# TensorE's fixed issue order, ended after the first part of a Conformer layer or kept to the end of the kernel

## The chip, the core and the metric

The kernel runs on one NeuronCore of one Trainium2 chip. The metric is the device time of one execution in microseconds. Three runs before the change gave 2952.1, 2952.1 and 2953.67 us; their median is 2952.1 us.

## What is computed

One inference step of a one-layer streaming encoder, in float32, for a prompt of 2048 frames and a sample of 64 frames (2112 rows, 1024 channels). Cut to what matters here:

```python
h = rms_norm(x, p['norm1_g']) * (1 + sc1) + sh1
z = h @ p['w_in']                                   # first part, with the convolution
...                                                 # and the band attention
conv_out, conv_state = conv_module(u, conv_hist, ..., p['w_conv_out'])
attn_out = o @ p['w_attn_out']
merged = jax.nn.sigmoid(g_conv) * conv_out + jax.nn.sigmoid(g_attn) * attn_out
x = x + gt1 * (merged @ p['w_o'])
h2 = rms_norm(x, p['norm2_g']) * (1 + sc2) + sh2
gate, up = jnp.split(h2 @ p['w_ffn_in'], 2, axis=-1)
x = x + gt2 * ((jax.nn.silu(gate) * up) @ p['w_ffn_out'])
```

The feed-forward width is 2816, which is 22 tiles of 128 channels (NF = 22). Everything from `conv_out` on is the second part of the kernel, and the change concerns this part.

## The kernel before

**Precision.** Every float32 operand of a product is split into a high and a low part (`whi` and `wlo` for weights), and one product is three TensorE matmuls (`mm3`: high x high, high x low, low x high). ScalarE copies the high part, VectorE or GpSimd subtracts to get the low part.

**Two parts.** The first part runs over four blocks of tokens and does the input projection, the convolution and the attention. The second part runs over three blocks of tokens, `CBLOCKS` = rows 0 to 576, 576 to 1344 and 1344 to 2112; they are called s = 0, 1, 2 below. For each block it does, in the order in which the program is written:

- *merge*, in two chunks of two or three token tiles: for each of eight channel tiles, 12 matmuls on the convolution branch and 12 on the attention branch (`ps<-cin` in the profile), then the gates on VectorE and the split into `m`.
- *output projection* (`wo`), after the merge of each chunk: `pw<-m`, per token tile 8 steps of 6 matmuls.
- *residual*, one Python generator per token tile: residual addition, norm, eight TensorE transposes (`pw<-ident,xn` or `pt<-ident,xn`), modulation ("columns"), and then the differences of the four quarters (channel halves x token halves) that the next stage uses. The quarters and their differences are tiles named b11, b21, b22 and t1 to t4; the profile leaves numbers out and calls them `b` and `t`. For the last chunk of block 0 (`by_pe`), three of the additions per tile are done by TensorE, two matmuls each, with a plus or minus identity matrix (`pw<-b,signs`).
- *feed-forward, first product*, as a product of two-by-two blocks with seven sub-products (Strassen's scheme): each of the 22 steps `up(f)` has seven groups of 12 matmuls. For f under 5 (EARLY) two of them are done ahead, in ten groups called `first(f)` and `second(f)`, which read b11 and b21. In `up(f)` the groups come in the order s2 x t2, s3 x t3, s1 x t1, a22 x t4 (all `ps<-t`), then a12 x b21, a11 x b11 of the next f, s4 x b22 (all `ps<-b`). For f = 0, s3 comes before s2.
- *feed-forward, second product*: `pd<-hid` and `pd<-sums`. In blocks 1 and 2 it is in seven sub-products too (`down_pair`, four stages D1 to D4 of 9, 18, 27 and 9 matmuls, one stage after each `next(between)` in `up(f)` for even f), elsewhere plain (`add_down`).

**What sets the order.** The program is written with a tile framework. Before it emits instructions, the framework's scheduler goes through all of them with a timing model and sets the order on each engine: of the instructions that the model holds ready, it takes the one that stands first in the program. Inside `tc.manual_schedule(engines={PE})` it keeps TensorE's instructions in the order of the program and orders only the other engines. On the chip each engine then works through its own list, and waits at an instruction whose operands or whose buffer aren't ready.

The program itself also has a planner, `Stream`: it adds up estimated times per engine (`stream.load`), and `spend()`, called at the end of each `mm3`, lets waiting generators step once their due time is reached (a *lane*; the residual generators are in the lane `turns`, at most one step in 600 ns of estimated TensorE time, two generators open at a time). So the transposes of the residual stand in the program between matmuls of other groups, at places that depend on the planner's estimates. At some points the program drains a lane, that is, emits all that is left in it at once. The place that matters most, in the second part of each block:

```python
for step, f in ((first, 0), (first, 1), (second, 0), (first, 2), (second, 1)):   # L2312
    step(f)
while hs["columns"]:                       # some tile's transposes not emitted yet
    turns.step(turns.gens[0])
W.presum()
if not s:
    W.begin_last()
turns.drain()                              # L2319
W.early = False
for step, f in ((first, 3), (second, 2), (first, 4), (second, 3), (second, 4)):  # L2321
    step(f)
    W.fill()
```

`first(0)`, `second(0)` and `first(2)` use the same PSUM bank (y0), `first(1)` and `second(1)` the bank z0, `first(3)` and `first(4)` banks of the ring of four called gp.

All instructions go through one helper that records them, so the profile shows nearly all of them at line 105; groups are told apart by tile names.

Of the kernel before, what the change touches and what calls it, by code (L numbers as in the profile page):

```python
# [622 lines left out]
def streaming_layer(ctx: ExitStack, tc: tile.TileContext, I, O):  # L623
# [1017 lines left out]
    ordered = ExitStack()  # L1641
# [68 lines left out]
    tail.drain()  # L1710
    stream.flush()
    side.close()
    ordered.close()
    p1.close()


# [185 lines left out]
    for s, (lo, hi) in enumerate(CBLOCKS):  # L1902
# [344 lines left out]
        def add_left(left):  # L2247

            for dst, x1, out in left:
                gps.tensor_tensor(dst, dst, x1, ALU.add)  # L2250
                stream.at(stream.when("pool") + OUT_LAG, lambda out=out, dst=dst: nc.sync.dma_start(out, dst))
                yield stream.when("pool"), {"pool": 500}
# [95 lines left out]
        stream.flush()  # L2348
        if left:
            work.add(add_left(left))  # L2350


_INS = [
# [26 lines left out]
```

## Time and profile before

| | us |
|---|---|
| median of three runs | 2952.1 |
| profiled execution, device time | 2952.32 |
| its span from first to last instruction | 2950.5 |
| TensorE busy in the span | 2890.8 (98%) |
| VectorE, ScalarE, GpSimd busy | 2046.4, 1363.3, 1162.6 |
| first matmul of the second part | at 1174.4 |
| last matmul | at 2944.8 |

Busy time counts a matmul to its modelled end, and successive matmuls overlap; the distance from one start to the next is the better measure of what a matmul takes in a row. "Idle before" an instruction, with an arrow to what released it, is a wait of the engine itself.

### The profile page before, as it was taken

How to read it: one execution, taken by the hardware profiler on the slowest of the kernel's cores; microseconds unless marked ns; L12 is line 12 of the kernel's file. 1: busy time of each engine (PE TensorE's matmuls, PEld its weight loads, DVE VectorE, ACT ScalarE, POOL GpSimd, SP SyncE). 2: the span in 40 equal slices, each digit the busy share in tenths (PEclk: the TensorE clock that was granted, in tenths of full speed). 3: DMA queues.
4: the chain of work that ended last, by engine and by line, in shares of the span. 5: the costliest groups of instructions: out<-in, count | busy, mean ns of one | idle time of the engine just before them, and what ended most of it. 6: DMA issues, size and time to landing. Idle time of an engine off the chain costs nothing.

```text
span 2950.5 us, 44832 instructions
## 1 busy us (share of the span) xinstructions
PE 2890.8 (98%) x16193; PEld 2585.3 (88%) x16193; DVE 2046.4 (69%) x3648; ACT 1363.3 (46%) x2453; POOL 1162.6 (39%) x753
## 2 busy tenths in 40 slices
PE   7999999999999999999999999999999999999999
PEld 5899777887888788888999998999999999999998
DVE  5897788667956885577767746666666557566666
ACT  3345533751465267464334345444444345444442
POOL 1101210111011002454566452366667742465667
PEclk9999999999999999999999999999999999999999
DMA  9989889978995997985444876332333965333333
GB/s 320 316 296 309 279 280 326 295 234 294 290 294 195 308 264 238 282 301 166 143 147 143 277 258 218 96 123 87 114 121 104 337 224 181 97 98 109 115 107 126
DMA packets 467067, 628.04 MB, mean 213 GB/s; under 512 B 36196, under 2 KB 314584, under 8 KB 466845
## 3 DMA queue, kind: packets, MB, share of 16 engines
q1 hardware_dynamic: 452944, 606.11, 63.6%
q10 hardware_dynamic: 13901, 19.08, 1.9%
q8 instruction: 127, 2.08, 0.3%
q14 instruction: 95, 0.78, 0.1%
HBM read 476.53 MB, written 148.54 MB: 212 GB/s over the span
## 4 chain that ended last, share of the span: by engine, by line
PE 46%; DVE 2%; DMA 1%; ACT 1%; issue 1%; POOL 0%; SPq 0%; ACTq 0%; DVEq 0%; POOLq 0%
PE ps L105 28%; PE pd L105 13%; PE pw L105 5%; DVE wlo L105 1%; ACT whi L105 0%; DVE ps L105 0%; DMA cin<-o_d 0%; DMA x<-x_d 0%; DMA wst<-in_w_conv_out 0%; POOL wlo L105 0%; DMA wfo<-in_w_ffn_out 0%; DVE acc L105 0%; DVE sums L105 0%; DVE pw L105 0%; DMA tg<-g_d 0%
## 5 line engine op out<-in xcount | busy, mean ns | idle before, releaser
L105 PE MATMUL ps<-t,whi 128*128 128x384 f32 (+1 forms) x2112 | 501.8, 322 | 3.2 <-DVE u L105 1.1
L105 POOL TENSOR_TENSOR wlo<-wst,whi 128x1024 fp32r<-128x1024 f32 (+1 forms) x159 | 363.4, 2297 | 235.0 <-ACT whi L105 213.6
L105 ACT ACTIVATE whi<-wst 128x1024 fp32r<-128x1024 f32 (+1 forms) x265 | 258.3, 979 | 317.0 <-PE ps L105 127.8
L105 PE MATMUL ps<-b,whi 128*128 128x384 f32 (+1 forms) x1584 | 380.6, 325 | 5.4 <-DVE v L105 2.1
L105 PEld LDWEIGHTS ps<-t,whi 128*128 128x128 f32 x2112 | 367.7, 188 | 10.5 <-ACT u L105 3.3
L105 DVE SCALAR_TENSOR_TENSOR y<-u,wd,y 128x512 f32<-128x512 f32 (+1 forms) x480 | 369.4, 773 | 7.2
L105 PE MATMUL ps<-hh,whi 128*128 128x512 f32 (+2 forms) x992 | 362.6, 365 | 0.1
L105 DVE TENSOR_TENSOR acc<-acc,pd 128x512 f32<-128x512 f32 x482 | 322.0, 684 | 48.4 <-PE pd L105 45.9
L105 PE MATMUL ps<-hh,wlo 128*128 128x512 f32 (+2 forms) x992 | 344.9, 348 | 0.0
L105 PE MATMUL ps<-hl,whi 128*128 128x512 f32 (+2 forms) x992 | 344.3, 347 | 0.0
L105 PE MATMUL ps<-t,wlo 128*128 128x384 f32 (+1 forms) x1056 | 338.2, 321 | 0.0
L105 PE MATMUL pd<-whi,hid 128*128 128x512 f32 x912 | 297.5, 391 | 0.5 <-DVE hid L105 0.3
L105 PEld LDWEIGHTS ps<-b,whi 128*128 128x128 f32 x1584 | 276.8, 188 | 13.6 <-DVE v L105 3.2
L105 ACT ACTIVATE pr<-pr,sm 128x640 f32<-128x640 f32 (+2 forms) x272 | 201.8, 748 | 138.5 <-DVE sm L105 136.6
L105 PE MATMUL ps<-b,wlo 128*128 128x384 f32 (+1 forms) x792 | 256.0, 323 | 0.0
L105 POOL TENSOR_TENSOR r<-t,mhalf 128x1 f32<-128x1 f32 (+2 forms) x68 | 82.3, 1219 | 415.5 <-DVE t L105 383.2
L105 PEld LDWEIGHTS ps<-hh,wlo 128*128 128x128 f32 x992 | 186.4, 188 | 22.7
L105 DVE TENSOR_TENSOR wlo<-wst,whi 128x1024 fp32r<-128x1024 f32 (+1 forms) x106 | 135.6, 1283 | 101.4 <-ACT whi L105 96.8
L105 PEld LDWEIGHTS pd<-whi,hid 128*128 128x128 f32 x912 | 171.1, 188 | 36.9 <-DVE acc L105 1.4
L105 PEld LDWEIGHTS ps<-hh,whi 128*128 128x128 f32 x992 | 187.0, 188 | 18.0 <-issue 2.9
L105 PEld LDWEIGHTS ps<-hl,whi 128*128 128x128 f32 x992 | 187.4, 189 | 14.5 <-issue 1.7
L105 PEld LDWEIGHTS ps<-t,wlo 128*128 128x128 f32 x1056 | 198.1, 188 | 0.8
(233 smaller groups left out, 6299.0 us busy)
## 6 DMA issues: line engine op xcount, KB each, us to landing
whi<-w_din_h SPq DMA_DIRECT2D x72, 512.0 KB, 6.9
wlo<-w_din_l SPq DMA_DIRECT2D x72, 512.0 KB, 7.0
wst<-sum_d SPq DMA_DIRECT2D x131, 256.0 KB, 2.9
wfo<-in_w_ffn_out SPq DMA_DIRECT2D x64, 512.0 KB, 4.1
wmod<-in_w_ada SPq DMA_DIRECT2D x46, 512.0 KB, 9.4
sum_d<-ws SPq DMA_DIRECT2D x88, 256.0 KB, 2.1
wst<-in_w_ffn_in SPq DMA_DIRECT2D x85, 256.0 KB, 3.3
wst<-in_w_in SPq DMA_DIRECT2D x40, 512.0 KB, 6.9
```

The lines of the kernel that those rows point to most:

```text
L105: self.last = f(*args, **kw)
```

## The change

The scope in which TensorE keeps the order of the program was closed at the end of the first part; now it is closed at the end of the kernel. So from the first merge on, TensorE too gets its matmuls and transposes in the order in which the program emits them. The instructions themselves, their operands and their number stay as they are; the other engines are ordered by the scheduler as before.

```diff
     tail.drain()
     stream.flush()
     side.close()
-    ordered.close()
     p1.close()
...
         stream.flush()
         if left:
             work.add(add_left(left))
+    ordered.close()
```

`ordered` is the scope, entered before the first part:

```python
ordered = ExitStack()
ordered.enter_context(tc.manual_schedule(engines={mybir.EngineType.PE}))
```

## The prediction

> **What bounds the kernel now.** I read the page's totals first, then the busy time by stage, then who ended TensorE's idle time in the second part.
>
> ```profile
> span 2950.5 us, 44832 instructions
> PE 2890.8 (98%) x16193; PEld 2585.3 (88%) x16193; DVE 2046.4 (69%) x3648; ACT 1363.3 (46%) x2453; POOL 1162.6 (39%) x753
> PE 46%; DVE 2%; DMA 1%; ACT 1%; issue 1%; POOL 0%; SPq 0%; ACTq 0%; DVEq 0%; POOLq 0%
> ```
> ```profile
> 1174.00:2951.00 1777.00, 1756.41 (x9682) 1626.11 (x9682) 1162.08 (x1934) 792.30 (x1375) 1001.78 (x601) 1.00 0.51 166
> 2000.00:2300.00 300.00, 300.00 (x1580) 281.43 (x1578) 196.03 (x320) 132.68 (x226) 205.30 (x124) 1.00 0.38 117
> ```
> ```profile
> PE ps L105 <- DVE t L105: 2.7, 4, 1.6
> PE ps L105 <- DVE v L105: 2.1, 3, 1.4
> ...
> PE pd L105 <- DVE acc L105: 0.3, 1, 0.3
> ```
> ```profile
> 2944.78 0.39 PE L105 MATMUL pd<-whi,hid 128*128 128x512 f32 x1
> ```
>
> TensorE bounds it. In the second part (first window row; first number after the comma is TensorE's busy time) it is idle for 1777.0 - 1756.4 = 20.6 us, and some 6 us of that lie behind the last matmul (last row). The waits before it are twelve small groups of 0.3 to 2.7 us (first two and last shown). Over 300 us of the feed-forward of block 1 it is never idle. So the change cannot save more than about 15 us, and the question is where the order of the trace differs from that of the program, since a matmul that ran ahead of its turn ran where TensorE would have waited.
>
> **The change part by part.** I compared the trace's sequence of tile names with the code. No work is added or removed; only the place of some matmuls changes.
>
> *Steady feed-forward: nothing.* In blocks 1 and 2 the trace has the program's groups in the program's order, down to one matmul of a22 x t4 that runs ahead of the second half of stage D2:
>
> ```profile
> 2004.26 0.33 PE L105 MATMUL ps<-t,whi 128*128 128x384 f32 x1
> 2004.43 0.39 PE L105 MATMUL pd<-whi,sums 128*128 128x512 f32 x1
> ```
>
> This moves 0.17 us behind instead of ahead, with no wait seen at either place. The transposes of the residual in these blocks stand after whole `mm3` triples, as the planner puts them, so they do not move either.
>
> *Block 0, merge: +1.1 us.* While a merge product waits for VectorE to free its bank, the trace runs five matmuls of the output projection (first two of five, then the released product), and three more from 1203.42 (the first of them):
>
> ```profile
> 1199.80 0.40 PE L105 MATMUL pw<-whi,m 128*128 128x512 f32 x1
> 1200.03 0.41 PE L105 MATMUL pw<-wlo,m 128*128 128x512 f32 x1
> 1201.58 0.54 PE L105 MATMUL ps<-cin,whi 128*128 128x320 f32 x2 [0.44 <-DVE m L105]
> ...
> 1203.42 0.40 PE L105 MATMUL pw<-wlo,m 128*128 128x512 f32 x1
> ```
>
> Start to start such a matmul takes 0.23 us. In program order it comes after the merge; the product still starts at 1201.58, so five fill nothing any more: 5 x 0.23 = 1.1 us. Ends: 0 (VectorE gets there sooner) and 8 x 0.23 = 1.8.
>
> *Block 0, residual of the last chunk: +9 us, the largest term.* Two tiles, A and B, each go through eight transposes, columns, and three additions by TensorE with VectorE and ScalarE work between them. The trace hides these chains under the 120 `first`/`second` matmuls (the 128 of the row are those and 8 additions) and under `up(0)`:
>
> ```profile
> 1287.20:1309.10 21.90, 19.40 (x128) 1.00 1.04 378
> ```
> ```profile
> 1294.36 1.14 ACT L105 ACTIVATE xn<-x,r 128x1024 f32<-128x1024 f32 x1
> 1297.52 1.58 PE L105 MATMUL pw<-ident,xn 128*128 128x128 f32 x13
> 1302.01 0.63 PE L105 MATMUL pw<-b,signs 128*128 128x512 f32 x2
> 1303.97 0.74 PE L105 MATMUL pw<-b,signs 128*128 128x512 f32 x2
> 1306.26 0.63 PE L105 MATMUL pw<-b,signs 128*128 128x512 f32 x2
> 1306.99 0.63 PE L105 MATMUL pw<-b,signs 128*128 128x512 f32 x2
> 1309.19 0.63 PE L105 MATMUL pw<-b,signs 128*128 128x512 f32 x2
> 1311.64 0.63 PE L105 MATMUL pw<-b,signs 128*128 128x512 f32 x2
> 1316.15 0.40 PE L105 MATMUL ps<-t,whi 128*128 128x288 f32 x1 [1.13 <-DVE u L105]
> 1419.27 0.30 PE L105 MATMUL ps<-t,wlo 128*128 128x288 f32 x1
> 1419.40 0.29 PE L105 MATMUL ps<-b,whi 128*128 128x288 f32 x1
> 1420.23 0.53 PE L105 MATMUL ps<-t,whi 128*128 128x288 f32 x2 [0.54 <-ACT u L105]
> ```
>
> The program does not interleave them so. Following the planner's sums by hand (it counts 288/2.4 ns per matmul, so 0.36 us per triple, and lets one residual step go at each tick), I find A's transposes after about 48 of the first 60 `b` matmuls and B's not yet emitted when the 60 are out. Then the loop on `hs["columns"]` emits all that is left of A, then B's transposes, and `turns.drain()` B's additions; only then come the other 60. A matmul of 288 takes 1419.40 - 1419.27 = 0.13 us. So: A's transposes when `xn` is there at 1295.5, the first 60 out at about 1298.1; A's first addition 2.9 us after its transposes (as from 1299.10 to 1302.01 in the trace), at 1299.4; the second 2.0 and the third 2.3 us later (1302.01, 1303.97, 1306.26), at 1303.7; B's transposes until 1305.2; its additions at 1308.1, 1310.3 and 1312.7 (1306.99, 1309.19, 1311.64); the other 60 until 1321.1; two groups of `up(0)`, 3.1 us, and a short wait for `u`: s1 x t1 starts at 1324.8. In the trace it starts at 1316.15 with 13 matmuls of `up(1)`, 1.7 us, already done. Loss: 8.7 + 1.7 = 10.4 us. If the chain's four steps between additions shrink to 1.5 us, since VectorE and ScalarE have less beside it, it is 7.4. I take 9. Ends: 3.5, if B's transposes do fall within the first 60 (saves 3.9 us), and 12, if A's don't either.
>
> *The clock after that: +3 us.* In these 15 us TensorE would work some 4 us. Once in the trace it was as little loaded:
>
> ```profile
> 1170.40:1173.80 3.40, 2.26 (x13) 1.58 (x11) 1.33 (x3) 1.94 (x4) 2.36 (x1) 1.00 0.29 114
> 1173.80:1180.60 6.80, 6.16 (x23) 6.16 (x24) 3.02 (x5) 1.88 (x3) 0.00 (x0) 0.50 0.63 233
> ```
>
> After 3.4 us with 2.26 us of busy time the granted clock (third number from the end) is 0.50 for 6.8 us. The same behind the drain halves up to 6.8 us of the second 60, 3.4 us lost, and stretches the additions by some 1.5 us: between 0 and 5, I take 3, since 4 in 15 is well below 2.26 in 3.4. [...]
>
> *Odd steps of block 0: +0.9 us.* The last three rows of the fence above show one a12 matmul running where s1 waits for `u`. It happens seven times; in program order each wait is longer by 0.13 us: 0.9. Ends 0 and 1.5.
>
> *Blocks 1 and 2, step 0: +4.3 us.* Here s1 x t1 waits until VectorE, busy with the residual, has made `u`:
>
> ```profile
> 1849.10:1860.25 11.15, 11.10 (x64) 1.00 0.40 130
> 1849.15 0.52 PE L105 MATMUL ps<-t,whi 128*128 128x384 f32 x2
> 1854.87 0.55 DVE L105 TENSOR_TENSOR u<-ps,early 128x384 f32<-128x384 f32 x1
> ```
>
> 64 `t` matmuls run there, 48 of `up(0)` and 16 of later steps. In program order s3 and s2 end at 1849.15 + 24 x 0.174 = 1853.3 and the next one starts after 1855.4: 2.15 us in each block, 4.3 together (0.174 is 11.10 / 64). Before that the trace runs `second(1)` ahead of `first(2)`, and `second(2)` ahead of `first(3)`; moving 12 matmuls back costs up to 2.1 us each time. I cost that at nothing, because VectorE's backlog sets 1855.4 anyway; without this cover it is 4.2 us more per block. Ends for both blocks: 2 and 6.
>
> *Blocks 1 and 2, step 4: +2.1 us.* Five `t` matmuls run while the second half of D2 waits for VectorE's additions:
>
> ```profile
> 1918.20:1919.42 1.22, 1.05 (x5) 1.00 0.01 2
> 1918.62 1.87 DVE L105 TENSOR_TENSOR acc<-acc,pd 128x512 f32<-128x512 f32 x3
> ```
>
> 5 x 0.174 = 0.87, and about 0.2 at D4 of the same step: 1.05 per block, 2.1 in all; ends 0 and 2.5.
>
> Sum: 1.1 + 9 + 3 + 0.9 + 4.3 + 2.1 = 20.4 us on the profiled execution's 2952.3: 2972.7. The median of the runs, 2952.1, is the same within 0.2 us. The low ends add to 5.5 us, the high ends to 28.8.
>
> **Rivals.**
> *The waits add up (slower still).* The swaps at `first(2)` and `first(3)` are not covered: 2 x 4.2 us, and the clock halves behind each, 2 x 3.4. That makes 20.4 + 15.2 = 35.6 us, 2988. For it speaks that VectorE is close to full there; against it, that its backlog was the limit.
>
> *No difference.* My placing of A and B by hand is wrong, and the program spreads the chains as the trace does. Then 5 to 8 us remain without the two large terms, and VectorE, relieved, gives a part back: about 2955. Here belongs also that the scope might not act on what was emitted behind a closed pool.
>
> *Faster.* With TensorE's order given, the scheduler lays out the other engines anew, and may put the copies that TensorE waits for first. The place: the odd steps of block 0, where ScalarE makes `u` so late that s1 waits 0.54 us behind one filling matmul, and the other eleven wait groups. The price: of the 15 us at most, half, 7 us, so 2945. It decides only where the two tiles' chains do not stand exposed, since they alone cost more. That TensorE waits for ScalarE in the trace speaks for it; that ScalarE and VectorE get no earlier input from a TensorE that never runs ahead speaks against it.
>
> **How the numbers follow.** About 0.2%, 5.9 us, is what a measurement can tell here from no change. Forecast 0.78, waits adding up 0.08, no difference 0.08, faster 0.06. So slower 0.86, same 0.08, faster 0.06. The range goes from the low ends, 2957, to the high ends and a little of the first rival, 2984; it leaves out about 0.2.
>
> **What would show it.** Right: `pw<-b,signs` at 1300 to 1313 stand alone, with idle time before them released by DVE and ACT, and 60 `ps<-b` of 288 come behind the last of them; the clock is 0.50 there; the 300 us from 2000 (shifted) stay at 300 busy; `ps<-t` of block 1 has a wait of about 2 us <-DVE u. Wrong: `b` groups still lie between the additions, or the idle time of the feed-forward's steady steps rises above zero, where I cost nothing.

## The result and the profile after

The changed kernel takes 2993.66 us (median of four runs, 2989.01 to 2996.25), the kernel before 2952.89 us beside it. The ratio is 1.0136, with a 95% interval of 1.0124 to 1.0148. So the loss is 40.8 us where 20.4 were forecast: the direction was right, the time lies 9.7 us above the range. The profiled execution of the changed kernel took 2989.01 us; its span is 36.7 us longer than before.

The page's totals, and two stages of the view by windows (after the comma TensorE's busy time; third number from the end the granted clock):

```profile
span 2987.2 us, 44844 instructions
PE 2899.0 (97%) x16193; PEld 2593.8 (87%) x16193; DVE 2052.1 (69%) x3648; ACT 1365.5 (46%) x2453; POOL 1160.3 (39%) x753
PE 46%; DVE 2%; DMA 1%; ACT 1%; issue 1%; POOL 0%; SPq 0%; DVEq 0%; ACTq 0%; POOLq 0%
```
```profile
1174.00:2987.00 1813.00, 1764.78 (x9682) 1633.58 (x9682) 1167.07 (x1934) 794.28 (x1375) 999.80 (x601) 0.99 0.50 163
2025.00:2325.00 300.00, 300.00 (x1580) 281.73 (x1579) 198.19 (x322) 133.92 (x230) 202.99 (x123) 1.00 0.35 110
```

The number of matmuls is the same. TensorE's busy time in the second part grows by 8.4 us, which fits a lower clock with the same matmuls (three matmuls of 288 take 0.72 us from start to start at half clock, from 1292.54 on, and 0.40 at full clock, from 1297.18 on), and its idle time grows from 20.6 to 48.2 us. The 300 us of steady feed-forward are as full as before. The waits of TensorE in the second part (total, times, longest, in us):

```profile
PE ps L105 <- DVE t L105: 7.9, 3, 5.9
PE ps L105 <- DVE early L105: 7.8, 3, 3.0
PE pw L105 <- DVE pw L105: 6.1, 2, 3.1
PE ps L105 <- DVE u L105: 5.9, 3, 2.6
PE pw L105 <- DVE t L105: 3.8, 3, 1.4
...
PE ps L105 <- ACT u L105: 2.2, 7, 0.7
```

The first two rows are new in size (2.7 and 0.9 us before) and are what the prediction did not have: a wait of 5.9 us ahead of a `b` group, and three ahead of `first(2)`.

**Where the time went.** Starts of the same groups in the two profiled executions, from their timelines:

| start of | before | after | difference |
|---|---|---|---|
| first merge matmul of block 0 | 1174.4 | 1174.3 | -0.1 |
| first `b` matmul of block 0 | 1287.2 | 1291.7 | +4.5 |
| first merge matmul of block 1 | 1687.6 | 1712.8 | +25.2 |
| first `b` matmul of block 1 | 1823.7 | 1849.0 | +25.3 |
| first `down_pair` matmul of block 1 | 1874.1 | 1903.6 | +29.5 |
| first merge matmul of block 2 | 2315.4 | 2346.7 | +31.3 |
| first `b` matmul of block 2 | 2453.5 | 2483.9 | +30.4 |
| first `down_pair` matmul of block 2 | 2503.9 | 2538.5 | +34.6 |
| end of the span | 2950.5 | 2987.2 | +36.7 |

Block 0 costs 25.2 us (14.0 forecast), the heads of blocks 1 and 2 cost 4.2 us each (2.15 forecast), the rest of them 1.8 and 2.1 us (1.05 forecast); the merge of block 2 is 0.9 us shorter.

**The head of block 0**, on TensorE's timeline (start, duration; in brackets the idle time before and its releaser), and what VectorE finished last before the first `b` matmul:

```profile
1285.36 0.39 PE L105 MATMUL pw<-whi,m 128*128 128x512 f32 x1
1291.68 0.82 PE L105 MATMUL ps<-b,whi 128*128 128x288 f32 x2 [5.93 <-DVE t L105]
...
1300.67 0.53 PE L105 MATMUL ps<-b,whi 128*128 128x288 f32 x2 [1.74 <-DVE early L105]
...
1303.93 1.04 PE L105 MATMUL pw<-ident,xn 128*128 128x128 f32 x8
1308.01 0.74 PE L105 MATMUL pw<-b,signs 128*128 128x512 f32 x2 [3.04 <-DVE pw L105]
1309.76 0.76 PE L105 MATMUL pw<-b,signs 128*128 128x512 f32 x2 [1.02 <-DVE t L105]
1311.93 1.22 PE L105 MATMUL pw<-b,signs 128*128 128x512 f32 x2 [1.41 <-DVE t L105]
1312.95 1.91 PE L105 MATMUL pw<-ident,xn 128*128 128x128 f32 x8
1317.94 2.58 PE L105 MATMUL pw<-b,signs 128*128 128x512 f32 x4 [3.08 <-DVE pw L105]
1321.93 1.22 PE L105 MATMUL pw<-b,signs 128*128 128x512 f32 x2 [1.41 <-DVE t L105]
1322.95 0.68 PE L105 MATMUL ps<-b,whi 128*128 128x288 f32 x2
...
1338.83 0.53 PE L105 MATMUL ps<-t,whi 128*128 128x288 f32 x2 [2.63 <-DVE u L105]
```
```profile
1291.25 0.29 DVE L105 TENSOR_TENSOR t<-pt,t 128x128 fp32r<-128x128 f32 x1
```

After the last matmul of the output projection TensorE stands still for 5.9 us. The operation that ends this reads `pt`: it belongs to the last difference made by the third tile of the first chunk, which reaches over the middle of the block's rows and whose transposes lie in the banks y0 and z0, those of `first(0)` and `first(1)`. Then come 60 `b` matmuls, all of A, all of B, and only then the other 60: from 1303.93 to 1322.95, 19.0 us, TensorE has nothing but the 16 transposes and 12 additions.

**The clock** in that stretch and behind the wait in block 1, with the 3.4 us ahead of each:

```profile
1286.49:1289.90 3.41, 0.00 (x0) 0.00 (x0) 3.41 (x4) 2.30 (x5) 3.10 (x3) 0.99 1.04 413
1289.90:1296.70 6.80, 5.02 (x21) 5.05 (x22) 1.79 (x6) 3.80 (x7) 2.35 (x3) 0.50 1.07 382
1303.50:1306.90 3.40, 1.47 (x13) 1.23 (x11) 1.99 (x5) 2.75 (x7) 2.19 (x3) 1.00 0.21 87
1306.90:1310.30 3.40, 1.27 (x4) 0.59 (x4) 3.04 (x4) 2.15 (x4) 1.66 (x2) 1.00 0.22 51
1310.30:1327.40 17.10, 11.06 (x36) 8.51 (x36) 6.87 (x13) 6.32 (x12) 0.00 (x0) 0.50 0.33 113
1856.50:1859.90 3.40, 0.44 (x2) 0.45 (x3) 3.40 (x7) 3.40 (x6) 0.95 (x1) 1.00 1.03 423
1859.90:1863.30 3.40, 3.40 (x13) 3.40 (x12) 3.40 (x6) 1.09 (x3) 1.43 (x1) 0.50 0.40 140
```

**The heads of blocks 1 and 2** have two waits each, of the same length in both blocks:

```profile
1859.46 0.68 PE L105 MATMUL ps<-b,whi 128*128 128x384 f32 x2 [3.02 <-DVE early L105]
...
1882.74 0.59 PE L105 MATMUL ps<-t,whi 128*128 128x384 f32 x2 [1.61 <-DVE u L105]
...
2494.32 0.67 PE L105 MATMUL ps<-b,whi 128*128 128x384 f32 x2 [3.02 <-DVE early L105]
...
2517.61 0.59 PE L105 MATMUL ps<-t,whi 128*128 128x384 f32 x2 [1.61 <-DVE u L105]
```

The first is `first(2)`, which waits for bank y0; the second is s1 x t1, which waits for `u`.

### The profile page after: what moved, and what is told of

It is laid out like the page before. It is cut to its first block, busy times and chain, and to the rows that moved or that the text cites. A ratio compares the mean times of both kernels' runs of the same rounds, so it can differ in the third digit from the quotient of the medians.

```text
span 2987.2 us, 44844 instructions
## 1 busy us (share of the span) xinstructions
PE 2899.0 (97%) x16193; PEld 2593.8 (87%) x16193; DVE 2052.1 (69%) x3648; ACT 1365.5 (46%) x2453; POOL 1160.3 (39%) x753
## 4 chain that ended last, share of the span: by engine, by line
PE 46%; DVE 2%; DMA 1%; ACT 1%; issue 1%; POOL 0%; SPq 0%; DVEq 0%; ACTq 0%; POOLq 0%
PE ps L105 28%; PE pd L105 13%; PE pw L105 5%; DVE wlo L105 1%; DMA wst<-in_w_attn_out 0%; ACT whi L105 0%; DVE acc L105 0%; DVE ps L105 0%; DMA wup<-in_w_conv_out 0%; DMA x<-x_d 0%; DMA cin<-c_d 0%; DVE pw L105 0%; DVE sums L105 0%; PE pt L105 0%; DMA wst<-sum_d 0%
```

## The experiments

The times below are medians. Kernels of one group ran on one chip, with the kernel before beside them: 2952.0 us with the first four, 2952.7 with the second, 2953.1 with the third and 2955.4 with the last two. The changed kernel's 2993.66 us come from a group of their own. In the profiles the first merge matmul starts between 1172.4 and 1180.2 us, so the first part alone, whose instructions are the same in all of them, varies by several us; where it matters I add a distance between two starts of one profile.

### Which place costs how much

**Head of block 0 free, the rest in order.** From the drain ahead of `first(0)` to the end of `up(1)` in block 0 the scheduler is free again.

```diff
+        if not s:
+            ordered.close()
         turns.drain([gen for gen, (t, _) in zip(groups[0] + groups[1], tiles) if t - lo < half])
...
             up(f + 1, ops, iter(()))
+            if not s and not f:
+                ordered.enter_context(tc.manual_schedule(engines={mybir.EngineType.PE}))
```

> TensorE's order is the program's in the whole second part, but for the stretch of block 0 from the first `first(0)` to the end of `up(1)` (the two tiles' chains and the 120 b matmuls), which the scheduler orders freely. My theory now: by the two traces 26 of the 37 us arise in this stretch, 4.2 us in the same stretch of blocks 1 and 2 each, 1.2 us in step 4 of both, some 2 us elsewhere. So it expects 11 to 14 us over the kernel before, 2964 to 2967. Rival (the other engines' new order costs all along, the stretch only shows it): 2980 or more.

Measured: 2969.85 us, ratio 1.0061 [1.0046, 1.0076]. That is 23.8 us less than the changed kernel (of another group), and 3 us above the range that I expected.

**Only the head of block 0 in order**, everything else in the second part free (the same two places, scope opened and closed the other way round).

> The converse: only that stretch of block 0 is in the program's order, all the rest of the second part is free. Theory: 24 to 28 us over the kernel before, 2977 to 2981. Rival that the loss is spread: under 15 us over, below 2968.

Measured: 2977.13 us, ratio 1.0085 [1.0070, 1.0100], 25.1 us over the kernel before. Both ways the head of block 0 costs 24 to 25 us, about twice the 12 that the prediction had there, and it costs this without any order elsewhere.

**The heads of all three blocks free** (the first diff without its `not s`).

> TensorE ordered in the second part, but for the heads of the three blocks: from the drain ahead of first(0) to the end of up(1) the scheduler is free. Theory (nearly all the loss is in the three heads): what is left is the merge (about 0), the odd steps of block 0 (1.0 us), step 4 of blocks 1 and 2 (2 x 1.2 us) and about 1 us at the end: 2956 to 2962. Rival (the free head of block 0 left 18 us, and the order elsewhere costs as much as it seemed to there: what a head loses is lost again at the next place where VectorE is behind): 2966 or more.

Measured: 2961.72 us, ratio 1.0034 [1.0021, 1.0047]. The heads of blocks 1 and 2 therefore cost 2969.85 - 2961.72 = 8.1 us, and 9.0 us are left for all the rest.

**Only the feed-forward in order**, from the end of `up(1)` to the end of each block, merge and heads free.

```diff
             up(f + 1, ops, iter(()))
+            if not f:
+                ordered.enter_context(tc.manual_schedule(engines={mybir.EngineType.PE}))
...
             work.add(add_left(left))
+        ordered.close()
```

> The kernel before, with TensorE ordered only from the end of up(1) to the end of each block: the steady feed-forward, the odd steps of block 0, step 4 of blocks 1 and 2 and the last products. The free heads run left 9 us, of which I can name 4.4 in these places. Theory (steady feed-forward nothing, odd steps 1.0, step 4 2 x 1.2, ends about 1): 2955.5 to 2958.5, the rest of the 9 us being the merge, the output projection and the first part's own variation. Rival (all of the 9 us lie here, so that the steady feed-forward is not free): 2960 to 2963.

Measured: 2959.17 us (seven runs from 2956.44 to 2966.72), ratio 1.0028 [1.0017, 1.0040]; that is between the two ranges. The profiled execution, the shortest of the seven, took 2956.44 us. That is 4.1 more than that of before, with the first merge matmul at 1174.3 us against 1174.4, and it is what the theory had. Its three largest waits in this stretch; before they were 0.8, 2.1 and 0.3 us, so the second is not new:

```profile
PE ps L105 <- ACT u L105: 2.3, 7, 0.7
PE ps L105 <- DVE v L105: 2.3, 3, 1.5
PE pd L105 <- DVE acc L105: 2.1, 2, 1.0
```

Where the other 2 us of the median come from, these runs do not tell.

### What costs it in the head of block 0

**Other banks.** `first(0)` and `first(1)` go to banks of the ring gp, as the third tile of the first chunk holds y0 and z0.

```diff
-            x = bank(("y0", "z0", "y0", "gp", "gp")[f])
+            x = bank((("y0", "z0", "y0", "gp", "gp") if s else ("gp", "gp", "y0", "z0", "y0"))[f])
```

> The changed kernel with one edit: in block 0, first(0), first(1) use gp banks and first(2) to first(4) the banks y0, z0, y0, since the tile that lies across the two halves holds y0 and z0 until its last differences are made, and the first b matmul waits 5.93 us for it. Theory: this wait goes, the first three groups run at 1286 to 1291, tile A's transposes come some 9 us earlier, and one of the two stretches at half clock goes: 8 to 12 us less than the changed kernel, 2982 to 2986. Rival (the wait only moves, since the two tiles' chain sets the end): within 3 us of the changed kernel.

Measured: 2986.72 us (2977.59 to 2989.73), ratio 1.0111 [1.0087, 1.0135], so 7 us less by the medians, though the runs spread over 12 us and the interval overlaps that of the changed kernel. From the last `pw<-m` of block 0 to the first `pd<-hid` this profile takes 60.6 us; the changed kernel takes 69.6, and three other profiles with the same head 68.5 to 70.9. No wait stands ahead of the `b` groups any more, but the chain of A and B is as it was:

```profile
1299.47 1.04 PE L105 MATMUL pw<-ident,xn 128*128 128x128 f32 x8
1304.47 2.58 PE L105 MATMUL pw<-b,signs 128*128 128x512 f32 x4 [3.97 <-DVE pw L105]
...
1318.45 1.22 PE L105 MATMUL pw<-b,signs 128*128 128x512 f32 x2 [1.41 <-DVE t L105]
```

**All 120 `b` matmuls ahead of the drain**, for the planner to spread A and B over them.

```diff
+        if not s:
+            for step, f in ((first, 3), (second, 2), (first, 4), (second, 3), (second, 4)):
+                step(f)
         while hs["columns"]:
...
```

(In block 0 this also drops the `W.fill()` after each of these five steps, which splits weights ahead.)

> The changed kernel with one edit: in block 0 the second 60 b matmuls are emitted ahead of the drain of the residual, so that the planner can put the two tiles' transposes and additions between them. Theory (the exposed serial chain is what costs): the 8 us of these matmuls, and up to 2 us of half clock on them, come under the chain: 6 to 10 us less than the changed kernel, 2984 to 2988. Rival: the planner's places are so early that TensorE stands at each addition as before, within 3 us of the changed kernel.

Measured: 2994.27 us, ratio 1.0143 [1.0128, 1.0158]: nothing gained, as the rival said. The planner spreads nothing here. A's transposes stand behind all 120, and the whole chain is bare:

```profile
1314.42 1.03 PE L105 MATMUL pw<-ident,xn 128*128 128x128 f32 x8
1320.26 1.22 PE L105 MATMUL pw<-b,signs 128*128 128x512 f32 x2 [4.80 <-DVE pw L105]
...
1334.94 1.22 PE L105 MATMUL pw<-b,signs 128*128 128x512 f32 x2 [1.41 <-DVE t L105]
```

The planner's own sums, read out of the program, say why. When block 0's head begins, its sum for TensorE stands at 1145.3 us, that for ScalarE at 1151.2. A's norm step is due when ScalarE is, at 1153.9; the 60 matmuls are out at 1152.5, so the drain takes all of A. With 120 ahead, the next due time, GpSimd's at 1166.3, lies behind these too (they are out at 1159.7). (These are the program's estimates and no times of the chip.)

**A and B placed by hand**, with the other banks. The automatic steps of the lane are off in block 0's head, and the program calls them between the groups (A(4): up to A's transposes, A(5) to A(8): its additions and what follows them; B the same).

```diff
+            first(0), first(1), A_(1), second(0), first(2), A_(2), B_(1), second(1), A_(3), B_(2)
+            first(3), B_(3), second(2), A_(4), first(4), A_(5), B_(4), second(3), A_(6), B_(5), second(4), A_(8), B_(8)
...
```

(The same edit moves `W.presum()` and `W.begin_last()` behind the ten groups and calls `W.fill()` once.)

> TensorE ordered throughout; in block 0 first(0) and first(1) are on banks of gp (as in the run with other banks, 2986.7 us), and the steps of the two tiles A and B are put by hand between the ten groups: A's transposes after 84 of the 120 b matmuls, B's after 96, A's and B's additions one after another behind those, instead of everything of A and B after 60. Theory (the loss in block 0's head is the exposed chain of A and B and the clock that falls in it): of some 14 us of idle time in that chain about 5 stay, and the half clock is short: 9 to 17 us less than with the banks alone, 2970 to 2978. Rival (in program order VectorE and ScalarE cannot keep up with the ten groups and the two tiles at once, wherever the transposes stand, as the run with all 120 ahead gained nothing): 2982 or more.

Measured: 2971.99 us (2965.61 to 2976.61), ratio 1.0066 [1.0053, 1.0079]. That is 14.7 us below the kernel with the banks alone, and 2 us above the one whose head is left to the scheduler. `b` groups now lie in the chain, and the bare waits are shorter:

```profile
1301.66 1.03 PE L105 MATMUL pw<-ident,xn 128*128 128x128 f32 x8
...
1307.34 1.22 PE L105 MATMUL pw<-b,signs 128*128 128x512 f32 x2 [2.25 <-DVE pw L105]
...
1314.07 0.73 PE L105 MATMUL pw<-b,signs 128*128 128x512 f32 x2 [1.60 <-DVE pw L105]
...
1318.97 0.73 PE L105 MATMUL pw<-b,signs 128*128 128x512 f32 x2 [1.66 <-DVE t L105]
```

So by the medians the 23.8 us of this head are about 7 us of bank, 14.7 us of chain with the clock that falls in it, and 2 that stay. The distance from the last `pw<-m` to the first `pd<-hid` splits it otherwise: 69.6 us in the changed kernel, 60.6 with other banks, 49.9 by hand and 46.4 with the head free, so 9.0, 10.7 and 3.5. One profile stands for each; both parts are there, their sizes are known to a few us.

### What costs it in blocks 1 and 2

**The two exchanges written into the program**, for blocks 1 and 2 alone.

```diff
-        for step, f in ((first, 0), (first, 1), (second, 0), (first, 2), (second, 1)):
+        for step, f in ((first, 0), (first, 1), (second, 0), (second, 1), (first, 2)) if s else ...
...
-        for step, f in ((first, 3), (second, 2), (first, 4), (second, 3), (second, 4)):
+        for step, f in ((second, 2), (first, 3), (first, 4), (second, 3), (second, 4)) if s else ...
```

> TensorE ordered throughout, as in the changed kernel (2993.7 us), but in blocks 1 and 2 the program itself issues second(1) ahead of first(2) and second(2) ahead of first(3), as the scheduler did in the kernel before. Theory (the bank y0 that first(2) reuses is held until ScalarE's silu of second(0), and nothing covers it): the wait of 3.0 us ahead of first(2) in each of the two blocks goes, and with it the 3.4 us at half clock behind it (1.7 us lost), while the wait of s1 x t1 for u stays at 1.6 to 3 us: 2 x 2 to 2 x 4 us less, 2985.5 to 2990. Rival (VectorE's backlog sets when u is there whatever comes before, as the prediction had it): the wait moves on to s1 x t1, which then waits 4 to 5 us, and the time stays at 2992 to 2995.

Measured: 2987.70 us (2984.41 to 2993.53), ratio 1.0123 [1.0107, 1.0139], 6 us below the changed kernel of another group; the two intervals overlap. In the profile of block 1 the 3.02 us are down to 0.47, and s1 x t1 does not wait longer but shorter, 0.74 instead of 1.61:

```profile
1864.84 0.62 PE L105 MATMUL ps<-b,whi 128*128 128x384 f32 x2 [0.47 <-DVE early L105]
...
1884.92 0.58 PE L105 MATMUL ps<-t,whi 128*128 128x384 f32 x2 [0.74 <-DVE u L105]
```

From the first `b` matmul of block 1 to the first `down_pair` matmul it takes 51.4 us instead of 54.6 (50.4 before), and the clock is 1.00 over these. s1 x t1 still waits for VectorE, but it starts 30.5 us after the first `b` matmul instead of 33.7: VectorE's backlog is not what sets its time whatever comes before. That a TensorE which isn't held up gives VectorE its input earlier would explain the shorter second wait; no run separates this.

**Both together**: A and B by hand in block 0, the exchanges in blocks 1 and 2.

> Both together: block 0 by hand as in the kernel of this call that does that, and the exchanged groups in blocks 1 and 2. Theory: the two gains add, 4 to 8 us less than block 0 by hand alone, so 2963 to 2973; if all the remaining terms were as counted (1.0 in the odd steps, 2.4 in step 4, 3 for u in blocks 1 and 2, 5 in the chain), 2952.9 + 11.4 = 2964. Rival (the savings do not add, as VectorE's backlog returns at the next place): within 3 us of block 0 by hand alone.

Measured: 2966.97 us, ratio 1.0050 [1.0037, 1.0062]. The gains add: 5.0 us less than by hand alone, on the same chip. The intervals overlap, but block 1 again takes 51.4 us from the first `b` to the first `down_pair` matmul, where by hand alone it takes 54.6.

### The clock by itself

**Fillers in the kernel with other banks.** Matmuls that nobody reads, in the waits of the chain.

```diff
-                def add(dst, sign, name):
+                def add(dst, sign, name, fill=0):
+                    d = bank("z0") if fill else None
+                    for q in range(fill):
+                        nc.tensor.matmul(d[:, :half], signs[0][:, 0], hs["b11"][0][:, q % 4, :half], start=True, stop=True)
...
-                add(b[0], 1, "b11")
+                add(b[0], 1, "b11", 18)
```

> The kernel with other banks in block 0 (TensorE ordered throughout, 2986.7 us), with matmuls added whose result nobody reads: 18 of 288 columns (0.13 us each) ahead of each tile's first addition, 5 and 8 ahead of the later ones, to a bank that is free there. They do nothing but keep TensorE busy in the waits of the chain of A and B. Theory (the half clock in that stretch, 17.1 us in the profile of that kernel, comes from the low load and costs what the additions and the first groups of the other 60 lose in it, some 3 us): the stretch is gone or below 7 us, and the time is 2981.5 to 2985. Rival (the halving follows from something else, or costs nothing because it lies in waits): the clock is still 0.50 for over 10 us there, or it is not and the time still is 2986 to 2990.

Measured: 2986.46 us (2978.79 to 2989.51), ratio 1.0110 [1.0097, 1.0124]. The half clock is gone from this stretch of the profile, but the median is that of the kernel without fillers (2986.72, in another group), and both spread over 11 us. The medians decide nothing on the size. In the two profiles the distance from the last `pw<-m` to the first `pd<-hid` is 58.0 us with fillers and 60.6 without: 2.6 us for this stretch.

**Fillers in the changed kernel**, 40 more of them in the wait of 5.9 us, and **the changed kernel beside it**, on one chip.

> The changed kernel with matmuls added whose result nobody reads, in the waits of block 0's head: 40 of 256 columns between the output projection and the first b group, where TensorE waits 5.9 us, and in the chain of A and B 18, 5 and 8 of 288 columns ahead of each tile's additions. Theory (the 6.8 and the 17.1 us at half clock in that head come from the low load, and cost what is worked in them: 2.5 us in the first 60 groups, 2.0 in the other 60, some 2.3 in the additions): both stretches are gone from the profile, and the time is 5 to 8 us below that of the changed kernel in this call. Rival (the halving costs nothing, since the waits absorb it): within 2 us of it.

> The changed kernel unaltered, beside the one with the added matmuls on the same chip: 2989 to 2996.

Measured: 2987.56 us (2980.75 to 2988.76) with fillers, ratio 1.0110 [1.0092, 1.0129]; 2992.57 us (2989.62 to 2994.91) without, 1.0127 [1.0108, 1.0145]. The difference of the medians is 5.0 us; the intervals of the two ratios overlap, while every run with fillers is below every run without. From the first `b` matmul to the first matmul of `down`, without fillers and with them:

```profile
1293.10:1356.00 62.90, 48.40 (x292) 44.04 (x293) 37.95 (x64) 28.86 (x56) 21.32 (x17) 0.83 0.59 199
```
```profile
1291.60:1348.80 57.20, 49.42 (x349) 46.56 (x350) 38.01 (x64) 28.71 (x56) 21.25 (x17) 1.00 0.64 218
```

The second has the 57 fillers of the chain more, its clock is 1.00 instead of 0.83, and it is 5.7 us shorter. From the last `pw<-m` on, so with the wait and its 40 fillers, it is 63.5 us instead of 68.5. Both stretches at half clock, 6.8 and 17.0 us in the first, are gone, and the mean clock of the span is 0.994 to 0.996 in the runs with fillers and 0.990 to 0.992 in those without. The other engines are ordered anew around the fillers; no run separates that from the clock.

### Can the order be written better?

**The chain earlier by hand**, with the exchanges: A's transposes after 60 instead of 84 `b` matmuls, B's after 84 instead of 96.

> TensorE ordered throughout, as block 0 by hand with the exchanged groups (2967.0 us), but with A's transposes after 60 instead of 84 of the 120 b matmuls, and B's after 84 instead of 96. Theory (what is left in that head is the part of the chain that no b matmul covers): with 12 to 24 more of them behind the transposes, 1.6 to 3.1 us less, 2963.5 to 2965.5. Rival (the chain is held by VectorE and ScalarE, which split weights between its steps; then the waits only move ahead): 2966.5 or more.

Measured: 2967.32 us, ratio 1.0048 [1.0036, 1.0060], against 2966.97: no gain, as the rival said. The waits have moved: `first(4)` now waits for the bank that `second(2)` has just used, and B's last addition for the differences of VectorE.

```profile
1307.07 0.53 PE L105 MATMUL ps<-b,whi 128*128 128x288 f32 x2 [1.30 <-DVE early L105]
...
1317.69 0.73 PE L105 MATMUL pw<-b,signs 128*128 128x512 f32 x2 [2.75 <-DVE t L105]
```

**The hand placement with the scheduler free**, on the kernel before.

> The kernel before (scheduler free in the second part), with the hand placement of A and B and the other banks in block 0. Theory (there the scheduler already puts the additions where their operands are there, so a program order that says so too can only take the 2 us of idle time at 1290.4 and 1316.2): 2950 to 2954. Rival (the steps emitted earlier go ahead of the groups' copies on VectorE and ScalarE, which keep a backlog there, and TensorE waits for the groups' banks): 2956 to 2962.

Measured: 2952.91 us (eleven runs), ratio 1.0004 [0.9995, 1.0013]: no difference. None of the versions beats the kernel before; the nearest with TensorE ordered in the heads too is 14 us slower.

## Why the prediction was half right

The prediction had the direction and the places, and half of the size. The three steps from the changed kernel to the kernel before set its terms beside the measured ones (medians of different groups; the sum is the whole loss by construction):

| place | forecast | measured | from |
|---|---|---|---|
| head of block 0 (chain, clock) | 12 | 23.8 | 2993.7 - 2969.9 |
| heads of blocks 1 and 2 | 4.3 | 8.1 | 2969.9 - 2961.7 |
| merge, odd steps, step 4, feed-forward | 4.1 | 9.0 | 2961.7 - 2952.7 |

More than half of what is missing lies in the head of block 0, 12 us in the sum and 23.8 measured.

**Block 0's chain (9 us): right in its mechanism, wrong in two steps.** The additions stand alone with waits released by VectorE, and the other 60 come behind the last of them, as the prediction said. The first step that failed is the place of A's transposes: I followed the planner by hand as if no engine had a backlog when the head begins, and put them after 48 matmuls; ScalarE's sum was 6 us ahead, and they come after all 60. The prediction had that as its "12" end. The second is a resource that was not in the sum at all: the banks y0 and z0 are used by the tile before A, and `first(0)` waits for its y0. The trace of before shows no such wait, because the scheduler put `first(1)`, on z0, first, then four matmuls of `first(3)`, `second(1)` and two more of `first(3)`, and `first(0)` only behind these 30 (the rows of the first and the 31st `b` matmul):

```profile
1287.24 0.43 PE L105 MATMUL ps<-b,whi 128*128 128x288 f32 x2
...
1292.60 0.53 PE L105 MATMUL ps<-b,whi 128*128 128x288 f32 x2
```

A swap that hides a wait hides also the reason for it. The run with other banks prices it at 7 us by the medians and 9 by the profiles.

**The clock (3 us, 0 to 5): right that it falls, low by some 2 us, at its upper end.** The fillers give 5.0 us for the two stretches, 2.6 of it by the profiles for the one that the prediction knew of; it had not seen the wait of 5.9 us that the other follows. The stretch of 17.1 us comes without a long gap: no wait near it exceeds 3.08 us, and in the 3.40 us ahead of it TensorE was busy for 1.27. The stretch of 6.8 us, by contrast, follows 3.41 us without a matmul, and so do, in the first part of the kernel before, 10.3 us at half clock, a place that the prediction's "once in the trace" left out:

```profile
388.70:392.10 3.40, 0.00 (x0) 0.00 (x0) 3.36 (x6) 0.22 (x1) 0.00 (x0) 1.00 0.66 207
392.10:402.40 10.30, 9.05 (x27) 7.65 (x28) 8.13 (x22) 4.39 (x13) 0.21 (x1) 0.50 0.98 337
```

How little work is enough, these traces don't tell: 1.47 us of busy time from 1303.50 to 1306.90 were followed by the full clock, 2.26 us in the prediction's row by the half. So the reason that the prediction gave, a lower busy share than in that row, is not a rule, and that it came out right for this stretch is partly luck. Nor do these traces show what sets a stretch's length: in the second part after the change they are 3.4, 6.8 and 17.1 us long, the two in block 0's head start 20.4 us apart, and the dip at 1173.8 us, 6.8 us long before, is 3.4 us long after, with 2.26 and 2.13 us of busy time in the 3.40 us ahead of it.

**Blocks 1 and 2, step 0 (4.3 us): the wrong half was priced.** "VectorE's backlog sets 1855.4 anyway" was the step that failed. The two exchanges, `second(1)` with `first(2)` and `second(2)` with `first(3)`, were costed at nothing; written into the program together they bring back 5.0 to 6.0 of the 8.1 us in two comparisons of medians, and 3.2 of the 4.2 us of block 1 in the profiles, and the wait for `u`, for which I had 4.3 us in both blocks, is 1.61 us in each. This is the mechanism of the rival "the waits add up", with the clock halved for 3.4 us behind it as the rival said; but the rival's 15.2 us were too much for it, and its total of 2988 came near the result by luck: the bank and the place of A in block 0 made up the rest.

**Odd steps (0.9), step 4 (2.1), merge (1.1), feed-forward (0).** In the profile the odd steps of block 0 show seven waits for `u` released by ScalarE, 2.2 us in sum (two and 0.8 before); step 4 and the rest of blocks 1 and 2 cost 1.8 and 2.1 us; the steady feed-forward is 300 of 300 us busy. The profiled execution with these alone in order is 4.1 us longer than before, against 3.0 forecast. The timed runs give 6.1 us for it, and 2.6 more for merge and output projection and the freed heads. Where these last 4 to 5 us come from is open. The profiles show no loss in the merge of block 0: from its first matmul to the last `pw<-m` it takes 111.1 us after and 112.6 before. The first part alone varies by more than 4 to 5 us between profiles.

**"No difference" and "faster"** did not come about: no version is faster than the kernel before beyond the noise (2952.91 against 2953.08 us at best). Whether the scheduler's new layout of the other engines gave something back that the waits hide, no run separates.

## What to carry to other kernels

When a scheduler has been free, its trace shows the order that avoids the waits and not the waits: before forcing the program's order, walk it and ask of every group which bank it reuses and who still reads that bank. A program order that is to be kept must carry the interleaving itself; written out by hand, three places (the banks, the steps of A and B, the exchanges) brought back 26.7 of the 40.8 us here. A due time computed from another engine's backlog moves a whole chain behind a drain when that backlog is a few us long, so read the planner's sums and don't assume them.

## What the hardware showed that I had not expected

The clock fell without a long gap, with no wait near it above 3.08 us, and busy time alone didn't tell when. A stretch of 3.4 us with 1.27 us of work was followed by 17.1 us at half clock, though TensorE was busy for 11.06 us of these; the stretch just ahead of it, with 1.47 us, was followed by the full clock. With matmuls put into the waits whose result nobody reads, the clock stayed up, and the kernel took 5.0 us less (2992.57 to 2987.56) while TensorE did more.
